# Full-height products in linear attention, later operands, and low parts of weights formed by accumulating transfers beside the key selection

## The chip, the cores and the metric

The kernel runs on one core of a Trainium2 chip. The metric is the device time of one execution in microseconds (us). In three runs the kernel before took 1966.81, 1968.53 and 1969.35 us; the median is 1968.53.

## The reference

Two transformer blocks are computed for 512 positions, in fp32. The change lies in the second block. Its input is normalized and multiplied by one wide weight matrix; the columns are q, k, v of sparse attention (qa, ka, va), the index queries and keys that select keys (qi, ki, wi), and q, k, v, the gates and the output gate of gated linear attention (qb, kb, vb, gdown, ogate).

```
score = einsum('bqhs,bqh->bqs', relu(q_idx . k_idx * c1), w_idx * c2)   # in blocks of 64 queries
_, sel = lax.top_k(score, 128)                                          # the key selection, 128 keys for each query
# gated linear attention, chunks of 64 positions, 4 heads, 64 key columns and 128 value columns each
q_in = q / 8 * exp(bcum);  k_in = k * exp(-bcum);  k_dec = k * exp(blast - bcum)
att  = tril(q_in . k_in) within a chunk
o    = att . v + q_in . state;   state = state * exp(blast) + k_dec^T . v
```

## The kernel before

**Products.** A weight product in fp32 is made of three (`mm3`): a tile of weights is split into a high part wh and a low part wl = raw - wh, and hi·hi (L160), hi·lo (L161) and lo·hi (L162) are accumulated in PSUM; the order of the operands on these lines makes L162 (L204 where tokens stand on the output's rows) the one that reads wl. `weights` (L167) loads a tile of 512 KB with an SP transfer into `raw`, ACT casts it to wh (L172), and a third engine subtracts (L173). raw, wh and wl have three buffers each, so a tile's buffers come back three tiles later. A tile feeds 24 products of 128 rows by 512 columns.

**The engine of the subtraction.** `low_engine["e"]` names it: VectorE (DVE), except from L1258 to L1267, during the key selection, where it is GpSimd (POOL).

**The key selection.** `topk_steps` makes index scores on TensorE (PE, L972, evacuated by ACT at L974 and weighted and added up by DVE at L977 and L979) and then runs rounds of max and match_replace on DVE (L989, L990) for three groups of 128 queries. Between its steps `bg.fill` takes steps of gemms out of a queue, in the order kb, vb, og, va, qk (`Feed`), so that PE has work while DVE selects. From the ninth step on, a generator, `gla_steps`, is advanced as well, one `next` for each step of the selection, as soon as the gemms that its last `yield` named are out of the queue.

**Linear attention.** Two heads share a tile: rows 0 to 63 belong to the one, rows 64 to 127 to the other. `gla_gates` makes the cumulated gates (L1072, L1074). `gla_operands(n)` makes q_in (in place, L1088), k_in and k_dec of pair n; `gla_turn(n)` transposes k_dec on PE (L1104) and copies it (L1106); `gla_inner(h)` makes the products inside chunks (L1135) and masks them; `gla_state` carries the states; `gla_out(h)` adds att·v (L1147, over 128 rows) and q_in·state (L1152, over the 64 rows of the head) in PSUM, in four blocks of one product of 128 columns and two of 64 (one in the first block).

**What sets the order.** The engines run their instructions in the order in which they are issued; the code is passed through a scheduler that orders each engine's instructions once, ahead of the run. A wait written after an instruction below holds everything behind it on that engine. Waits on DMASW are for transfers that POOL issues, those on DMAHW for transfers that SP issues.

Of the kernel before, what the change touches and what calls it, by code (L numbers as in the profile page):

```python
# [121 lines left out]
def build(tc, A, dump=None):  # L122
    nc = tc.nc
    with ExitStack() as es:
# [11 lines left out]
        def wtile(tag, shape, dt):  # L136
            return P.tile(shape, dt, tag=tag, name=tag, bufs=SLOTS[tag])
# [27 lines left out]
        low_engine = {"e": nc.vector}  # L165

        def weights(w, k0, kn, c0, ncol):  # L167
            raw = wtile("raw", [128, kn, ncol], F32)
            nc.sync.dma_start(raw, w[k0 * 128:(k0 + kn) * 128, c0:c0 + ncol].rearrange("(k p) n -> p k n", p=128))
            wh = wtile("wh", [128, kn, ncol], F32R)  # L170
            wl = wtile("wl", [128, kn, ncol], F32R)
            nc.scalar.copy(wh, raw)  # L172
            low_engine["e"].tensor_tensor(out=wl, in0=raw, in1=f(wh), op=ALU.subtract)  # L173
            return wh, wl
# [905 lines left out]
        def gla_operands(n, bc):  # L1080
            bl = small("bl", 8, bufs=2)
            nc.vector.tensor_copy(bl, bc[:, 63:T:64])
            eb = small("eb", 8, bufs=2)
            nc.scalar.activation(eb, bl, AF.Exp, scale=1.0 / 16)
            gl["eb", n] = eb
            e1 = new("t")
            nc.scalar.activation(e1, bc, AF.Exp, scale=1.0 / 16)
            nc.vector.scalar_tensor_tensor(out=qb[n], in0=qb[n], scalar=0.125, in1=e1, op0=ALU.mult, op1=ALU.mult)  # L1088
            e2 = new("t")
            nc.scalar.activation(e2, bc, AF.Exp, scale=-1.0 / 16)  # L1090
            kin = new("q")
            nc.vector.tensor_mul(kin, kb[n], e2)
            gl["k", n] = kin
            bc3 = bc.rearrange("p (c s) -> p c s", s=64)
            nc.vector.tensor_sub(bc3, bl[:, :, None].to_broadcast([128, 8, 64]), bc3)
            nc.scalar.activation(bc, bc, AF.Exp, scale=1.0 / 16)
            nc.vector.tensor_mul(kb[n], kb[n], bc)
# [30 lines left out]
                                                   in1=kv[rr, hh * 128:hh * 128 + 128], op0=ALU.mult, op1=ALU.add)  # L1128

        def gla_inner(h):  # L1130
            n, rr = h // 2, slice(64 * (h % 2), 64 * (h % 2) + 64)
            z = psum("r")
            for b in range(4):
                bs = slice(b * 128, b * 128 + 128)
                nc.tensor.matmul(z[:, bs], gl["k", n][rr, bs], qb[n][rr, bs], start=True, stop=True)  # L1135
            at = new("q")
            nc.gpsimd.memset(at, 0.0)
            nc.vector.copy_predicated(at, gl["mask"], z)
            gl["at", h] = at

        def gla_out(h):
            n, rr = h // 2, slice(64 * (h % 2), 64 * (h % 2) + 64)
            at = gl["at", h]
            o = psum("r")
            for b in range(4):
                bs = slice(b * 128, b * 128 + 128)
                nc.tensor.matmul(o[:, bs], vb[b][:, h * 128:h * 128 + 128], at[:, bs], start=True, stop=False)  # L1147
                for c in (2 * b, 2 * b + 1):
                    if c == 0:
                        continue  # L1150
                    s = gl["S", n][(c - 1) // 4][rr, ((c - 1) % 4) * 128:((c - 1) % 4) * 128 + 128]
                    nc.tensor.matmul(o[:, c * 64:c * 64 + 64], s, qb[n][rr, c * 64:c * 64 + 64], start=False,  # L1152
                                     stop=c == 2 * b + 1)
            oh = new("q")
            nc.scalar.copy(oh, o)
            gl["o", h] = oh
            sq = new("t")
            nc.scalar.activation(sq, o, AF.Square)
            st = psum("o")
            colsum(st, 0, [sq])  # L1160
            rc = small("rcg", 4, bufs=4)
            rsqrt_cols(rc, st[:, 0:4], 4, 1.0 / 128)
            gl["r", h] = rc
# [11 lines left out]
        def gla_steps():  # L1175
            bcs = []
            for _ in gla_gates(bcs):
                yield "start"
            glam = const(None, C_GLA, 512)
            gl["mask"] = small("glau", 512, U8)  # L1180
            nc.gpsimd.tensor_copy(out=gl["mask"], in_=glam)
            yield "kb"
            for n in range(2):
                gla_operands(n, bcs[n])
                yield "kb"
            for n in range(2):
                gla_turn(n)
                yield "kb"
            for h in range(4):
                gla_inner(h)  # L1190
                yield "vb"
            for c in range(7):
                for n in range(2):
                    gla_state(n, c)
                yield "vb"
            for h in range(4):
                gla_out(h)
                yield "og"
                if h > 0:
                    gla_norm(h - 1)  # L1200
            yield "og"
            gla_norm(3)
# [52 lines left out]
            for c in range(4):  # L1255
                yield from gemm(A["w_out_2"], 4, 256 * c, late, ev, n0=2 * c, k0w=4)
        bg.add("wo", residual())
        low_engine["e"] = nc.gpsimd  # L1258
        gla = gla_steps()
        wait = next(gla)  # L1260
        for i, us in enumerate(topk_steps()):
# [157 lines left out]
```

## Time and profile before

| what | value |
|---|---|
| median of three runs | 1968.53 us |
| the profiled execution | 1973.42 us |
| its span, from first to last instruction | 1971.7 us |
| mean granted TensorE clock | 0.978 of full speed |
| PE busy | 1893.1 us, 96% |
| DVE busy | 1071.8 us, 54% |
| ACT busy | 725.8 us, 37% |
| POOL busy | 315.9 us, 16% |

A busy PE is not PE at its best: its products take longer where the granted clock is lower, and a product that waits inside PE for the one before it counts as busy. The selection begins at about 1264 us, the first piece of `gla_out` runs at 1382 us, and the last head ends at about 1414 us.

### The profile page before, as it was taken

The page shows a single profiled execution, that of the slowest core. Times are in us where ns is not written, and L with a number is a line of the kernel's source. Part 1 is how long each engine was busy: PE and PEld are TensorE (multiplying, and loading weights), DVE is VectorE, ACT ScalarE, POOL GpSimd, SP SyncE. Part 2 cuts the span into 40 slices and gives each one's busy share as a digit, 9 for nine tenths or more (in the row PEclk, how much of TensorE's full clock was granted, in tenths as well). Part 3 has the DMA queues.
Part 4 walks back from the last instruction along what each step waited for, and adds up shares of the span by engine and source line. Part 5 has one row for each costly group of instructions (what it writes and reads, how often), then busy time and mean ns, then how long its engine had stood idle before and what let it go on. Part 6 is the DMA issues. An engine that isn't in the chain of part 4 may idle for free. (4 is left out here: it accounts for less than half of the span.)

```text
span 1971.7 us, 24556 instructions
## 1 busy us (share of the span) xinstructions
PE 1893.1 (96%) x9561; PEld 1572.9 (80%) x9561; DVE 1071.8 (54%) x1730; ACT 725.8 (37%) x1226; POOL 315.9 (16%) x357
## 2 busy tenths in 40 slices
PE   5889999999999999999999999979999899999998
PEld 4678887888889898888888888767878788888886
DVE  6788875645464554664443322587377653433222
ACT  3466654233323323343222223552256532322222
POOL 3232211112020302010000002332344200000000
PEclk8899999999999999999999999989899999999999
DMA  7612222443424243623323234232133123333222
GB/s 222 193 54 65 65 73 92 146 123 107 134 88 142 79 137 124 196 76 106 93 90 96 91 102 123 66 109 63 34 101 103 53 66 95 96 96 95 87 86 75
DMA packets 193520, 199.25 MB, mean 101 GB/s; under 512 B 9718, under 2 KB 178692, under 8 KB 193404
## 3 DMA queue, kind: packets, MB, share of 16 engines
q1 hardware_dynamic: 189920, 188.48, 31.2%
q0 software_dynamic: 3136, 9.08, 1.3%
q8 instruction: 75, 1.23, 0.3%
q14 instruction: 41, 0.34, 0.1%
q10 hardware_dynamic: 348, 0.13, 0.0%
HBM read 189.25 MB, written 9.99 MB: 101 GB/s over the span
## 5 line engine op out<-in xcount | busy, mean ns | idle before, releaser
L160 PE MATMUL ps_g<-p,wh 128*128 128x512 f32 (+1 forms) x1464 | 580.4, 399 | 9.5 <-ACT p L150 2.9
L161 PE MATMUL ps_g<-p,wh 128*128 128x512 f32 (+1 forms) x1464 | 577.3, 395 | 2.9 <-DVE p L405 2.9
L162 PE MATMUL ps_g<-p,wl 128*128 128x512 f32 (+1 forms) x1464 | 576.6, 394 | 0.0
L173 DVE TENSOR_TENSOR wl<-raw,wh 128x1024 fp32r<-128x1024 f32 (+1 forms) x262 | 325.7, 1243 | 448.3 <-ACT wh L172 447.1
L172 ACT CAST wh<-raw 128x1024 fp32r<-128x1024 f32 (+1 forms) x282 | 294.3, 1044 | 658.3 <-PE ps_g L161 373.2
L160 PEld LDWEIGHTS ps_g<-p,wh 128*128 128x128 f32 x1464 | 277.3, 190 | 74.6 <-issue 7.5
L161 PEld LDWEIGHTS ps_g<-p,wh 128*128 128x128 f32 x1464 | 278.1, 190 | 63.8 <-DVE p L405 3.6
L162 PEld LDWEIGHTS ps_g<-p,wl 128*128 128x128 f32 x1464 | 277.7, 190 | 63.2
L203 PE MATMUL ps_g<-wh,p 128*128 128x256 f32 x512 | 148.0, 289 | 1.6 <-ACT wh L172 1.5
L204 PE MATMUL ps_g<-wl,p 128*128 128x256 f32 x512 | 145.7, 285 | 1.2 <-DVE wl L173 1.2
L205 PE MATMUL ps_g<-wh,p 128*128 128x256 f32 x512 | 145.9, 285 | 0.0
L160 PE MATMUL ps_g<-q,wh 128*128 128x512 f32 (+1 forms) x368 | 141.7, 388 | 0.2 <-DVE p L1253 0.2
L162 PE MATMUL ps_g<-q,wl 128*128 128x512 f32 (+1 forms) x368 | 141.6, 385 | 0.0
L161 PE MATMUL ps_g<-q,wh 128*128 128x512 f32 (+1 forms) x368 | 141.5, 385 | 0.0
L203 PEld LDWEIGHTS ps_g<-wh,p 128*128 128x128 f32 x512 | 98.7, 193 | 3.0 <-ACT wh L172 1.9
L204 PEld LDWEIGHTS ps_g<-wl,p 128*128 128x128 f32 x512 | 98.8, 193 | 1.9 <-DVE wl L173 1.4
L205 PEld LDWEIGHTS ps_g<-wh,p 128*128 128x128 f32 x512 | 98.8, 193 | 0.1
L160 PEld LDWEIGHTS ps_g<-q,wh 128*128 128x128 f32 x368 | 69.1, 188 | 16.1 <-DVE p L1253 0.5
L162 PEld LDWEIGHTS ps_g<-q,wl 128*128 128x128 f32 x368 | 69.2, 188 | 15.0
L161 PEld LDWEIGHTS ps_g<-q,wh 128*128 128x128 f32 x368 | 69.2, 188 | 14.6
L150 ACT CAST q<-t 128x512 fp32r<-128x512 f32 (+1 forms) x68 | 39.2, 582 | 87.3 <-DVE t L880 48.8
L319 DVE SCALAR_TENSOR_TENSOR adaacc<-raw,cact,adaacc 128x256 f32<-128x256 f32 x112 | 53.8, 481 | 24.9 <-DMA raw<-in_w_ada 23.1
(373 smaller groups left out, 2601.0 us busy)
## 6 DMA issues: line engine op xcount, KB each, us to landing
raw<-in_w_in SPq DMA_DIRECT2D x108, 512.0 KB, 3.6
raw<-in_w_ffn_in SPq DMA_DIRECT2D x44, 512.0 KB, 3.5
raw<-in_w_ada SPq DMA_DIRECT2D x32, 512.0 KB, 3.4
raw<-in_w_ffn_gate SPq DMA_DIRECT2D x22, 512.0 KB, 3.7
raw<-in_w_ffn_up SPq DMA_DIRECT2D x22, 512.0 KB
raw<-in_w_ffn_down SPq DMA_DIRECT2D x22, 512.0 KB, 3.7
raw<-in_w_ffn_out SPq DMA_DIRECT2D x19, 512.0 KB, 3.4
raw<-in_w_proj_ret SPq DMA_DIRECT2D x16, 512.0 KB, 3.3
```

The lines of the kernel that those rows point to most:

```text
L150: nc.scalar.copy(hi, src)
L160: nc.tensor.matmul(ps, lh, rh, start=start, stop=False)
L161: nc.tensor.matmul(ps, lh, rl, start=False, stop=False)
L162: nc.tensor.matmul(ps, ll, rh, start=False, stop=stop)
L172: nc.scalar.copy(wh, raw)
L173: low_engine["e"].tensor_tensor(out=wl, in0=raw, in1=f(wh), op=ALU.subtract)
L203: nc.tensor.matmul(o, xh[:, ts], wh[:, i], start=k == 0 and t % 2 == 0, stop=False)
L204: nc.tensor.matmul(o, xh[:, ts], wl[:, i], start=False, stop=False)
L205: nc.tensor.matmul(o, xl[:, ts], wh[:, i], start=False, stop=k == KD - 1 and t % 2 == 1)
L319: nc.vector.scalar_tensor_tensor(out=acc, in0=w, scalar=c, in1=acc, op0=ALU.mult, op1=ALU.add)
```

## The change

Three things are changed. In the part of the program in which POOL subtracted, a low part is now formed so: ACT writes wh, ACT writes -wh into the buffer of wl, and a transfer issued by POOL adds raw to it. q_in of a pair is no longer one tile in place but two tiles of 128 rows, one for each head, in which the 64 rows of the other head are set to zero by POOL; `gla_inner` and `gla_out` then contract over all 128 rows. And `gla_steps` yields once more ahead of each `gla_operands`, so that operands, transposes and all that follows come one step of the selection later for the first pair and two for the second.

```diff
--- before.py
+++ after.py
@@ -165,6 +165,16 @@
         low_engine = {"e": nc.vector}
 
         def weights(w, k0, kn, c0, ncol):
+            if low_engine["e"] is None:
+
+                raw = wtile("raw", [128, kn, ncol], F32)
+                nc.sync.dma_start(raw, w[k0 * 128:(k0 + kn) * 128, c0:c0 + ncol].rearrange("(k p) n -> p k n", p=128))
+                wh = wtile("wh", [128, kn, ncol], F32R)
+                wl = wtile("wl", [128, kn, ncol], F32R)
+                nc.scalar.copy(wh, raw)
+                nc.scalar.activation(wl, f(wh), AF.Copy, scale=-1.0)
+                nc.gpsimd.dma_start(wl, raw, accum_op=ALU.add)
+                return wh, wl
             raw = wtile("raw", [128, kn, ncol], F32)
             nc.sync.dma_start(raw, w[k0 * 128:(k0 + kn) * 128, c0:c0 + ncol].rearrange("(k p) n -> p k n", p=128))
             wh = wtile("wh", [128, kn, ncol], F32R)
@@ -1085,7 +1095,12 @@
             gl["eb", n] = eb
             e1 = new("t")
             nc.scalar.activation(e1, bc, AF.Exp, scale=1.0 / 16)
-            nc.vector.scalar_tensor_tensor(out=qb[n], in0=qb[n], scalar=0.125, in1=e1, op0=ALU.mult, op1=ALU.mult)
+            for hh in range(2):
+
+                r, o = slice(64 * hh, 64 * hh + 64), slice(64 - 64 * hh, 128 - 64 * hh)
+                qz = gl["q", 2 * n + hh] = new("q")
+                nc.gpsimd.memset(qz[o], 0.0)
+                nc.vector.scalar_tensor_tensor(out=qz[r], in0=qb[n][r], scalar=0.125, in1=e1[r], op0=ALU.mult, op1=ALU.mult)
             e2 = new("t")
             nc.scalar.activation(e2, bc, AF.Exp, scale=-1.0 / 16)
             kin = new("q")
@@ -1128,18 +1143,18 @@
                                                    in1=kv[rr, hh * 128:hh * 128 + 128], op0=ALU.mult, op1=ALU.add)
 
         def gla_inner(h):
-            n, rr = h // 2, slice(64 * (h % 2), 64 * (h % 2) + 64)
+            n, qz = h // 2, gl["q", h]
             z = psum("r")
             for b in range(4):
                 bs = slice(b * 128, b * 128 + 128)
-                nc.tensor.matmul(z[:, bs], gl["k", n][rr, bs], qb[n][rr, bs], start=True, stop=True)
+                nc.tensor.matmul(z[:, bs], gl["k", n][:, bs], qz[:, bs], start=True, stop=True)
             at = new("q")
             nc.gpsimd.memset(at, 0.0)
             nc.vector.copy_predicated(at, gl["mask"], z)
             gl["at", h] = at
 
         def gla_out(h):
-            n, rr = h // 2, slice(64 * (h % 2), 64 * (h % 2) + 64)
+            n, qz = h // 2, gl["q", h]
             at = gl["at", h]
             o = psum("r")
             for b in range(4):
@@ -1148,8 +1163,8 @@
                 for c in (2 * b, 2 * b + 1):
                     if c == 0:
                         continue
-                    s = gl["S", n][(c - 1) // 4][rr, ((c - 1) % 4) * 128:((c - 1) % 4) * 128 + 128]
-                    nc.tensor.matmul(o[:, c * 64:c * 64 + 64], s, qb[n][rr, c * 64:c * 64 + 64], start=False,
+                    s = gl["S", n][(c - 1) // 4][:, ((c - 1) % 4) * 128:((c - 1) % 4) * 128 + 128]
+                    nc.tensor.matmul(o[:, c * 64:c * 64 + 64], s, qz[:, c * 64:c * 64 + 64], start=False,
                                      stop=c == 2 * b + 1)
             oh = new("q")
             nc.scalar.copy(oh, o)
@@ -1181,6 +1196,7 @@
             nc.gpsimd.tensor_copy(out=gl["mask"], in_=glam)
             yield "kb"
             for n in range(2):
+                yield "kb"
                 gla_operands(n, bcs[n])
                 yield "kb"
             for n in range(2):
@@ -1255,7 +1271,7 @@
             for c in range(4):
                 yield from gemm(A["w_out_2"], 4, 256 * c, late, ev, n0=2 * c, k0w=4)
         bg.add("wo", residual())
-        low_engine["e"] = nc.gpsimd
+        low_engine["e"] = None
         gla = gla_steps()
         wait = next(gla)
         for i, us in enumerate(topk_steps()):
```

Line numbers behind `weights` grow by 10, behind `gla_operands` by 15: L972 becomes L982, L1104 becomes L1119, L1135 becomes L1150, L1147 and L1152 become L1162 and L1167. The negation is L175, the accumulating transfer L176.

What the change does to the order of instructions is seen at three places. The first is PE at the beginning of the selection, with the first tile of the kb gemm (p are its activations). Before:

```order
L160 MATMUL ps_g<-p,wh 128x512 [waits DVE_49]
L161 MATMUL ps_g<-p,wh 128x512
L162 MATMUL ps_g<-p,wl 128x512 [waits Pool_49]
...
L161 MATMUL ps_g<-p,wh 128x512
L162 MATMUL ps_g<-p,wl 128x512
L160 MATMUL ps_g<-p,wh 128x512 [waits DVE_49,PE_49]
L972 MATMUL ps_z<-q 128x512 [waits DVE_49]
L972 MATMUL ps_r<-q 128x512 x2
L161 MATMUL ps_g<-p,wh 128x512
L960 MATMUL ps_o<-eye,q 128x8 [waits DVE_49]
L960 MATMUL ps_o<-eye,q 128x8 x2
L162 MATMUL ps_g<-p,wl 128x512
```

and now:

```order
L160 MATMUL ps_g<-p,wh 128x512 [waits DVE_49]
L161 MATMUL ps_g<-p,wh 128x512
L160 MATMUL ps_g<-p,wh 128x512 [waits DVE_49,PE_49]
L161 MATMUL ps_g<-p,wh 128x512
L982 MATMUL ps_z<-q 128x512 [waits DVE_49]
L982 MATMUL ps_r<-q 128x512 x2
...
L1225 MATMUL ps_o<-k,rel 8x384 [waits DMASW5_49,DMASW1_49,DVE_49]
L982 MATMUL ps_z<-q 128x512 [waits DVE_49]
L1069 MATMUL ps_o<-q,k 128x512 [waits DMASW6_49,DVE_49]
L160 MATMUL ps_g<-p,wh 128x512 [waits Activation_49]
L161 MATMUL ps_g<-p,wh 128x512
L162 MATMUL ps_g<-p,wl 128x512 [waits DMASW0_49]
```

Before, L162 stood third and waited for POOL's subtraction; now four products that do not read wl come first, then the index products and the two small products of L1225 and L1069, and the first L162 behind them waits for the transfer (DMASW0).

The second place is POOL in the same part (gd, far and gt are tables of the position bias). Before:

```order
L1215 DMA far<-gd 128x8x1 [waits DMASW2_49,DMASW0_49]
L1217 DMA gt<-gd 1032x1x384 [waits DMASW3_49]
L173 TENSOR_TENSOR wl<-raw,wh 128x1024 [waits DMAHW2_49,PE_49,Activation_49]
L236 DMA k<-in_consts 128x512 [waits DMASW6_49,DMASW4_49,PE_49]
L173 TENSOR_TENSOR wl<-raw,wh 128x1024 [waits DMAHW3_49,PE_49,Activation_49]
L173 TENSOR_TENSOR wl<-raw,wh 128x1024 [waits DMAHW4_49,PE_49,Activation_49]
L1277 DMA k<-gt 128x2x256 [waits DMASW3_49,DMASW1_49,DVE_49]
L1181 CAST glau<-k 128x512 [waits DMASW4_49]
L1277 DMA k<-gt 128x2x256 [waits Pool_49]
L173 TENSOR_TENSOR wl<-raw,wh 128x1024 [waits DMAHW5_49,PE_49,Activation_49]
L1137 MEMSET q 128x512 x4
L173 TENSOR_TENSOR wl<-raw,wh 128x1024 [waits DMAHW6_49,Activation_49]
```

and now:

```order
L176 DMA wl<-raw 128x1024 [waits DMASW3_49,DMAHW0_49,Activation_49,Pool_49]
L1231 DMA far<-gd 128x8x1 [waits DMASW4_49,DMASW2_49]
L1233 DMA gt<-gd 1032x1x384
L176 DMA wl<-raw 128x1024 [waits DMAHW1_49,DMASW6_49,Activation_49]
L176 DMA wl<-raw 128x1024 [waits DMASW7_49,DMASW0_49,DMAHW2_49,PE_49,Activation_49]
...
L176 DMA wl<-raw 128x1024 [waits DMASW3_49,DMASW1_49,DMAHW3_49,PE_49,Activation_49]
L1293 DMA k<-gt 128x2x256 [waits DMASW5_49,DVE_49]
...
L176 DMA wl<-raw 128x1024 [waits DMASW6_49,DMAHW4_49,DMASW4_49,Activation_49]
L1102 MEMSET q 64x512 x2
L176 DMA wl<-raw 128x1024 [waits DMASW7_49,DMAHW5_49,PE_49,Activation_49]
L1102 MEMSET q 64x512 x2
```

Subtractions are now issues of transfers; those of the first tiles stand among the transfers of gd, far and gt on the same queue, the third one behind gt, and the zeros of q_in (L1102) stand between later ones.

The third place is PE around the first transposes of linear attention, in the gemm of vb. Before:

```order
L203 MATMUL ps_g<-wh,p 128x256
L204 MATMUL ps_g<-wl,p 128x256 [waits Pool_49]
L205 MATMUL ps_g<-wh,p 128x256
L203 MATMUL ps_g<-wh,p 128x256
L204 MATMUL ps_g<-wl,p 128x256
L205 MATMUL ps_g<-wh,p 128x256
L1104 MATMUL ps_o<-eye,q 128x128 [waits DVE_49]
L1104 MATMUL ps_o<-eye,q 128x128 x3
```

and now, the first three rows at the place where the transposes stood and the others where they stand:

```order
L213 MATMUL ps_g<-wh,p 128x256
L214 MATMUL ps_g<-wl,p 128x256 [waits DMASW4_49]
L215 MATMUL ps_g<-wh,p 128x256
...
L213 MATMUL ps_g<-wh,p 128x256 [waits Activation_49]
L214 MATMUL ps_g<-wl,p 128x256 [waits DMASW5_49]
L215 MATMUL ps_g<-wh,p 128x256
L1119 MATMUL ps_o<-eye,q 128x128 [waits DVE_49]
L1119 MATMUL ps_o<-eye,q 128x128 x3
```

The transposes stand 46 rows later in PE's order (row 6275 in place of 6229; those of the second pair 6298 in place of 6252), behind the first product that waits for one tile more.

## Rows read from the trace of the kernel before

**Rows 1.** The page: busy us, share of the span and instructions of each engine.

```profile
PE 1893.1 (96%) x9561; PEld 1572.9 (80%) x9561; DVE 1071.8 (54%) x1730; ACT 725.8 (37%) x1226; POOL 315.9 (16%) x357
```

**Rows 2.** Waits of PE, 1255 to 1470 us: us in total, times, longest.

```profile
PE ps_z L972 <- ACT t L974: 8.1, 1, 8.1
PE ps_o L1104 <- DVE p L1106: 3.3, 1, 3.3
```

**Rows 3.** Stretches: length, busy us (instructions) of the engines, clock, DMA share, GB/s.

```profile
1275.00:1289.00 14.00, 14.00 (x32) 7.70 (x31) 5.10 (x9) 6.67 (x11) 7.83 (x6) 0.51 0.48 130
1300.00:1320.00 20.00, 11.86 (x49) 9.44 (x48) 20.00 (x33) 8.80 (x19) 9.97 (x7) 0.74 0.42 119
...
1392.00:1408.00 16.00, 16.00 (x84) 14.70 (x83) 2.63 (x6) 2.79 (x5) 2.87 (x3) 0.69 0.11 33
```

**Rows 4.** Timeline of PE: start us, us, engine line operation out<-in.

```profile
1382.34 0.38 PE L1147 MATMUL ps_r<-q,p 128*128 128x128 f32 x2
...
1386.02 0.50 PE L160 MATMUL ps_g<-p,wh 128*128 128x512 f32 x1
...
1387.51 0.95 PE L268 MATMUL ps_o<-ones,t 128*128 128x1 f32 x8
1388.32 0.48 PE L160 MATMUL ps_g<-p,wh 128*128 128x512 f32 x1
...
1336.96 1.16 PE L1135 MATMUL ps_r<-q 64*128 64x128 f32 x8
```

**Rows 5.** Groups of POOL, whole span: count, then busy us, mean ns, idle before.

```profile
L173 POOL TENSOR_TENSOR wl<-raw,wh 128x1024 fp32r<-128x1024 f32 x20 | 48.6, 2432 | 85.7 <-ACT wh L172 77.3 <-DVE q L956 8.3
```

**Rows 6.** Timeline of POOL, 1262 to 1335 us.

```profile
1299.43 2.40 POOL L173 TENSOR_TENSOR wl<-raw,wh 128x1024 fp32r<-128x1024 f32 x1 [13.80 <-ACT wh L172]
1301.79 0.58 POOL L236 DMA_DIRECT2D k<-in_consts  x1
1302.39 5.29 POOL L173 TENSOR_TENSOR wl<-raw,wh 128x1024 fp32r<-128x1024 f32 x2
```

**Rows 7.** Timeline of DVE, 1298 to 1330 us.

```profile
1297.54 0.69 DVE L1072 TENSOR_TENSOR t<-t 128x512 f32<-128x512 f32 x1 [2.09 <-ACT t L1069]
...
1299.93 2.99 DVE L1074 TENSOR_TENSOR_SCAN q<-k,t 128x512 f32<-128x512 f32 x1
...
1303.43 2.06 DVE L979 SCALAR_TENSOR_TENSOR q<-t,wi,q 128x384 f32<-128x384 f32 x1
...
1306.07 2.16 DVE L1072 TENSOR_TENSOR t<-t 128x512 f32<-128x512 f32 x1
...
1308.76 1.20 DVE L1074 TENSOR_TENSOR_SCAN q<-k,t 128x512 f32<-128x512 f32 x1
...
1311.90 0.59 DVE L979 SCALAR_TENSOR_TENSOR q<-t,wi,q 128x384 f32<-128x384 f32 x1
...
1322.48 2.51 DVE L1092 TENSOR_TENSOR q<-q,t 128x512 f32<-128x512 f32 x1 [0.74 <-ACT q L1040]
```

**Rows 8.** Timeline of ACT, 1262 to 1278 us.

```profile
1263.63 1.05 ACT L172 CAST wh<-raw 128x1024 fp32r<-128x1024 f32 x1
...
1274.30 1.05 ACT L172 CAST wh<-raw 128x1024 fp32r<-128x1024 f32 x1
```

**Rows 9.** DMA issues: count, KB each, median us from issue to landing.

```profile
yspill<-p POOLq DMA_DIRECT2D x8, 256.0 KB, 3.3
...
gt<-gd POOLq DMA_DIRECT2D x1, 1548.0 KB, 10.8
```

**Rows 10.** Timeline of PE, 1266 to 1283 us.

```profile
1268.23 0.40 PE L160 MATMUL ps_g<-p,wh 128*128 128x512 f32 x1
...
1270.80 0.40 PE L162 MATMUL ps_g<-p,wl 128*128 128x512 f32 x1
1272.55 0.47 PE L160 MATMUL ps_g<-p,wh 128*128 128x512 f32 x1 [1.35 <-DVE q L933]
...
1280.04 0.63 PE L160 MATMUL ps_g<-p,wh 128*128 128x512 f32 x1
```

## The prediction

> **What bounds the kernel now.** Read the page's share of busy time first [rows 1]: TensorE (PE) works 96% of the span, so time is won only where PE stands still, runs at its lower clock level, or spends longer on its products than it need. The change touches only the second block from the start of the key selection (about 1264 us) to the end of gated linear attention (about 1414 us); the rest of the program keeps its instructions. So the second view is the list of PE's waits in that stretch [rows 2]. Two of them stand where the change works. PE waits 8.1 us once in front of L972, the index products, for ACT's L974, which evacuates scores that VectorE (DVE) has not yet consumed; and 3.3 us once at L1104, the transposes of linear attention's k, for DVE's copies at L1106. The third view is a table of stretches [rows 3]. In 1275 to 1289 PE has work the whole time but a granted clock of 0.51, its lower level (1.2 of 2.4 GHz), after gaps at the start of the selection such as the one of 1.35 us before 1272.55 [rows 10]. In 1300 to 1320 DVE is busy 20.00 of 20.00 us: there the selection rounds set the pace and PE waits for them. In 1392 to 1408 PE is busy throughout, waits for nobody, and is granted 0.69. That stretch follows the first two heads of `gla_out`; what PE did before the clock fell was mostly full products with these short 64-row ones between them. The fourth view, the timelines, gives durations.
>
> **Products over all rows.** The pieces of `gla_out` for one head run from 1382.34 to 1386.02, where the next gemm product starts: 3.68 us [rows 4], for four products of 128 columns at L1147 and seven chunks of state products at L1152. L1152 contracts over 64 partitions and L1147 over 128, and they alternate. A run of fp32 products that do not alternate is L268: eight from 1387.51 to the next product at 1388.32, 0.10 us each, though with one column [rows 4]. An fp32 product counts twice in the trace: 8 for L1147 and 14 for L1152, 22 in a head. At 0.10 these take 2.2 us, so a head could lose 1.45 us and four heads 5.8. `gla_inner` (L1135, eight of 64 rows, 1.16 us before PE goes on at its pace) against L268 (0.95 for eight) adds 0.2 to 0.3 a head, some 1.1 in all. The spacing is worth 6.9 us, bounds 6.9 and 0, since no row shows the 128-row form of these very products, and L268's narrowness may flatter it. I take the upper end, because the products that follow one another without a change of rows are the nearest row. The clock of 1392 to 1408 has lost 16 x 0.31 = 5.0 us; if products that use half of the rows are what let it fall, full rows give most of it back. I take 4, bounds 0 and 5.0. Together 10.9.
>
> The trace shows a head's 3.68 us and not why it is long. The Trainium skill ("TensorE: Matmul & The Clock Gate", section "Why this matters for your kernels") says that one product with a small contraction takes as long as a full one, and that only several tiles running side by side gain; by that the spacing term would be 0. Its page "TensorEngine Tiling (Array Packing)", section "Key Properties", says that a change of tiling mode drains the engine; by that the alternation is the cost and the 6.9 stands. The alternating 22 at 0.17 us against 0.10 for L268 agree with the second, so I follow it and keep the first as a rival.
>
> **GpSimd's subtractions go.** Twenty at 2.43 us leave POOL [rows 5]. POOL is not on the path; DVE, which they slow, is. While POOL subtracts at 1299.43 and 1302.39 (two, 5.29 us) [rows 6], DVE's L1074 takes 2.99 us where its twin takes 1.20, L979 2.06 against 0.59, L1072 2.16 against 0.69 [rows 7]: 1.8 + 1.5 + 1.5 = 4.7 us before the 8.1 us wait ends. L1092 at 1322.48 is a `tensor_tensor` of the shape of L1072 and takes 2.51 against 0.69, which is 1.8 before the 3.3 us wait.
>
> **The longer way of a low part.** Cast, negation and an accumulating transfer replace cast and subtraction. The negation has the shape of the cast: 1.05 us [rows 8], 20 of them 21 us on ACT, which in 1300 to 1320 works 8.80 of 20 us [rows 3], so it is hidden there. POOL's issue costs 0.58 us (L236) [rows 6] in place of 2.43. No row shows an accumulation between two SBUF tiles. Bounds for its landing: 3.3 us for 256 KB and 10.8 us for 1548 KB, both on POOL's queue [rows 9]. Between them on a line, 512 KB give 4.8 us, and 7.8 if reading source and destination counts as 1024 KB; I take 6. Per tile that is 1.05 + 1.05 + 0.6 + 6 = 8.7 us from raw data to low part. A tile feeds 24 products at 0.233 us ((1270.80 - 1268.23) / 11) [rows 10], 5.6 us, and with three buffers of each kind two tiles, 11.2 us, cover it. So in the steady part it costs nothing; where cover lacks is the start and, perhaps, the third tile, whose transfer the order puts behind the 1548 KB of `gt` in POOL's queue: 0 if the queue overlaps them, up to about 6 if not; I take 2.
>
> At the start there is no cover. ACT is full of evacuations: the second cast comes 10.7 us after the first [rows 8], and in the new order the negation of tile one stands about there. Its transfer can leave at 1276 and lands at 1282. PE before has run 19 products of the first tile by 1280.04 (the twelfth at 1270.80) [rows 10]; in the new order it runs only four that need no low part, then waits at L162. Fifteen products are late: 15 x 0.233 = 3.5 us, or 7.0 at the lower level. The clock there is 0.51 [rows 3], so I take 6. What absorbs it: PE comes 6 us later to the 8.1 us wait, DVE 4.7 us earlier, together over 8.1, so the wait ends (-8.1) and the start's delay is paid (+6). If DVE's relief failed, the wait would only shrink by the 6 us and both would cancel. After this wait the next late thing is DVE itself, whose rounds are still 20 of 20 there.
>
> **Operands later and in halves.** Two more `scalar_tensor_tensor` of 64 rows: 2 x 0.68 = 1.4 us more on DVE (L1088's shape, as L1072's 0.69 [rows 7]; a half-height instruction is assumed to cost the same). Against the relief of 1.8 that leaves 0.4; but the two additional steps put each L1104 some 46 rows later in PE's order, more cover than the 3.3 us wait. New waits in front of `gla_inner` for POOL's zeros (four half tiles) have a POOL that has lost 48.6 us of work as cover. I count -1.8 of the 3.3, bounds -3.3 and +1.4.
>
> **Sum.** -6.9 - 4 + 6 - 8.1 - 1.8 + 2 = -12.8 us on the profiled execution (1973.4 us, span 1971.7): 1960.6. That execution lies 4.9 us above the median of the runs, 1968.5; with the same distance the median becomes 1955.7, forecast 1956.
>
> **Rivals.** (1) *The transfers are late for every tile, slower.* PE would meet its first low-part product before the landing. Three buffers turn over in three tiles, 16.8 us; a turn needs 5.6 (products) + 2.9 (cast, negation with its issue) + landing, so it decides from a landing of 8.3 us. At 10.8 a turn loses 2.5 us, 20 tiles lose 17, and each wait brings some of the lower clock, as after the gaps before 1275 (0.51): with 6 us for that +23, 1956 + 23 = 1979. For it: the accumulation moves twice the bytes, and `gt` shares the queue. Against: 3.3 us for a spill on that queue. POOL issued L236 at 1301.79 in 0.58 us, while DVE was fully busy [rows 3, 6]. The skill's page "SBUF — State Buffer", section "Who interferes with whom", says that a DMA issued by GpSimd can be starved by DVE's use of their shared port; that would bring this rival about in just the 20 us where DVE never rests, and the 0.58 us is against it. Chance 0.15.
> (2) *The wider products gain nothing.* Each takes what a 64-row product takes and the clock falls as before: 1956 + 10.9 = 1967. For it: L1152 and L1147 alternate columns and accumulation too, not rows alone. Chance 0.13.
> (3) *The start is paid and the waits stay.* The rounds on DVE go no faster, or other work waits for them: -10.9 + 6 = -4.9, 1964. For it: DVE is at 20.00 of 20.00 and gets two more instructions. Chance 0.13.
> (4) *Everything goes*: -6.9 - 5.0 - 8.1 - 3.3 = -23.3, with the start's late products filling other gaps: 1945. Chance 0.10.
> The forecast keeps 0.49, with a range of its own of 1951 to 1961.
>
> A measurement tells 0.2% (3.9 us) from no change: under 1964.6 is faster, over 1972.5 slower. Faster: the forecast 0.49, (4) 0.10, about 0.09 of (3), 0.03 of (2) = 0.71. Slower: nearly all of (1) = 0.15. Same: 0.14. The range 1947 to 1974 leaves out most of (1) and half of (4).
>
> **What would show it.** In the new profile a head of `gla_out` takes about 2.3 us instead of 3.68, and the clock between its heads stays near 1; if it takes 3.6, the product step is wrong. L1074 at 1.2 us throughout shows DVE's relief. The wait before L982 for ACT is gone or below 2 us, and one of some 3 to 7 us appears at the first L162, for the transfer. The accumulation lands in 4 to 8 us; above 8.3 us PE waits at L162 and L214 again and again, and the forecast is wrong. ACT's own queue must not become what L162 waits for beyond the first tile.

## The result, and the profile after

Four runs of the changed kernel took 1955.99 to 1957.54 us, median 1956.9; four of the kernel before, 1966.81 to 1969.35, median 1968.44. The ratio is 0.9938 (95% interval 0.9926 to 0.9950): faster by 11.5 us, where 12.5 were forecast (1956 us, range 1947 to 1974). A second measurement, told below, gave 0.9923 (0.9902 to 0.9943).

The profiled executions lie further apart: 1973.42 before and 1956.69 after, 16.7 us. That of before is 5.0 us above its median, that of after 0.2 below. Both traces are compared below, so what they show adds up to 16.7 and not to 11.5. All of it lies in the part that was changed: from the first product of the kb gemm to the first score product (L493, L503 now) of the attention that follows linear attention, PE takes 189.4 us before and 172.0 after, 17.4 less, while 0.2 us are lost ahead of this stretch and 0.6 behind it.

```profile
1457.65 0.34 PE L493 MATMUL ps_z<-q 128*128 128x128 f32 x2
```

```profile
1268.43 0.40 PE L160 MATMUL ps_g<-p,wh 128*128 128x512 f32 x1
...
1440.40 0.34 PE L503 MATMUL ps_z<-q 128*128 128x128 f32 x2
```

The first row is that of before, whose stretch begins at 1268.23 [rows 10]. In which stage the other executions of the kernel before were shorter than the profiled one is not recorded.

The page of the changed kernel, with busy time, share and instructions of each engine, against [rows 1]:

```profile
span 1955.0 us, 24601 instructions
...
PE 1879.9 (96%) x9561; PEld 1563.7 (80%) x9561; DVE 1062.4 (54%) x1732; ACT 748.5 (38%) x1248; POOL 287.9 (15%) x361
```

PE's share is unchanged; it lost 13 us of busy time with the same number of instructions. ACT has gained 23 us and 22 instructions: the 20 negations, and two more loads of its function tables (`ACT_TABLE_LOAD`, 1.28 us each; 9 in the trace instead of 7).

The waits of PE, 1255 to 1470 us, against [rows 2] (us in total, times, longest):

```profile
PE ps_z L982 <- ACT t L984: 6.6, 3, 3.1
PE ps_g L160 <- DVE q L943: 3.7, 1, 3.7
...
PE ps_r L982 <- ACT t L984: 1.2, 1, 1.2
PE ps_z L982 <- DVE q L964: 0.5, 1, 0.5
```

The wait for ACT's L984 (L974 before) is not gone: with 6.6 + 1.2 = 7.8 us it is nearly what it was, 8.1. The wait at the transposes of linear attention is gone, and so is one of before at L160, behind linear attention, that the rows ahead of the prediction do not have:

```profile
PE ps_g L160 <- DVE q L475: 2.6, 1, 2.6
```

No wait for a transfer appears.

Four stretches, against [rows 3] (length, busy us of PE, PEld, DVE, ACT, POOL, then clock, DMA share and GB/s):

```profile
1300.00:1320.00 20.00, 14.30 (x42) 10.60 (x43) 16.83 (x34) 13.47 (x27) 3.54 (x5) 0.66 0.59 155
1320.00:1340.00 20.00, 20.00 (x162) 19.47 (x161) 14.14 (x30) 8.48 (x12) 7.03 (x12) 1.00 0.73 151
...
1392.00:1408.00 16.00, 16.00 (x140) 15.79 (x139) 7.03 (x16) 6.47 (x11) 6.67 (x6) 1.00 0.26 62
1408.00:1438.00 30.00, 30.00 (x163) 25.64 (x162) 22.94 (x58) 16.19 (x22) 7.09 (x8) 1.00 0.74 168
```

DVE has 3.2 us free in 1300 to 1320. From 1320 to 1438 PE works without a gap and the clock is 1.00, its upper level, in every stretch read. The work that stood in 1392 to 1408 before, at a clock of 0.69, stands 6 to 12 us earlier now, and earlier, too, stands the work that follows the wait of 2.6 us, at 1423 in place of 1439. There the clock was 0.66 before:

```profile
1438.00:1443.00 5.00, 3.60 (x10) 2.93 (x11) 3.62 (x9) 2.75 (x4) 2.37 (x1) 0.66 0.00 0
```

The timeline of PE, against [rows 4]:

```profile
1378.71 0.38 PE L1162 MATMUL ps_r<-q,p 128*128 128x128 f32 x2
1378.93 0.33 PE L1167 MATMUL ps_r<-q 128*128 128x64 f32 x2
1379.10 0.44 PE L1162 MATMUL ps_r<-q,p 128*128 128x128 f32 x2
1379.38 0.56 PE L1167 MATMUL ps_r<-q 128*128 128x64 f32 x4
1379.77 0.44 PE L1162 MATMUL ps_r<-q,p 128*128 128x128 f32 x2
...
1381.09 0.48 PE L160 MATMUL ps_g<-p,wh 128*128 128x512 f32 x1
...
1339.81 1.05 PE L1150 MATMUL ps_r<-q 128*128 128x128 f32 x8
1340.62 0.37 PE L213 MATMUL ps_g<-wh,p 128*128 128x256 f32 x1
```

A head of `gla_out` takes 2.38 us instead of 3.68, and `gla_inner`'s eight products 0.81 us where the next product followed after 1.08. The DVE timeline, against [rows 7], and the landing of the new transfers, against [rows 9]:

```profile
1302.21 1.21 DVE L1084 TENSOR_TENSOR_SCAN q<-k,t 128x512 f32<-128x512 f32 x1
...
1305.11 0.68 DVE L1082 TENSOR_TENSOR t<-t 128x512 f32<-128x512 f32 x1
...
1306.36 1.22 DVE L1084 TENSOR_TENSOR_SCAN q<-k,t 128x512 f32<-128x512 f32 x1
```

```profile
wl<-raw POOLq DMA_DIRECT2D x20, 512.0 KB, 5.6
```

L1084 no longer takes 2.99 us, nor L1082 2.16. A low part lands 5.6 us after its issue, the median of the 20 (6 was taken).

### The profile page after: what moved, and what is told of

Read it like the earlier page. It is cut to its first block, busy times and chain, and to the rows that moved or that the text cites. A ratio compares the mean times of both kernels' runs of the same rounds, so it can differ in the third digit from the quotient of the medians.

```text
span 1955.0 us, 24601 instructions
## 1 busy us (share of the span) xinstructions
PE 1879.9 (96%) x9561; PEld 1563.7 (80%) x9561; DVE 1062.4 (54%) x1732; ACT 748.5 (38%) x1248; POOL 287.9 (15%) x361
## 5 line engine op out<-in xcount | busy, mean ns | idle before, releaser
L160 PE MATMUL ps_g<-p,wh 128*128 128x512 f32 (+1 forms) x1464 | 579.4, 399 | 9.3 <-DVE q L943 3.7
L162 PE MATMUL ps_g<-p,wl 128*128 128x512 f32 (+1 forms) x1464 | 575.5, 394 | 0.0
L182 ACT CAST wh<-raw 128x1024 fp32r<-128x1024 f32 (+1 forms) x262 | 273.2, 1043 | 630.5 <-PE ps_g L161 358.3
L160 PEld LDWEIGHTS ps_g<-p,wh 128*128 128x128 f32 x1464 | 276.4, 190 | 75.1 <-issue 8.3
L162 PEld LDWEIGHTS ps_g<-p,wl 128*128 128x128 f32 x1464 | 277.2, 189 | 63.4
L160 PE MATMUL ps_g<-q,wh 128*128 128x512 f32 (+1 forms) x368 | 141.7, 388 | 0.2 <-DVE p L1269 0.2
L162 PE MATMUL ps_g<-q,wl 128*128 128x512 f32 (+1 forms) x368 | 141.5, 385 | 0.0
L160 PEld LDWEIGHTS ps_g<-q,wh 128*128 128x128 f32 x368 | 69.1, 188 | 16.1 <-DVE p L1269 0.6
L162 PEld LDWEIGHTS ps_g<-q,wl 128*128 128x128 f32 x368 | 69.2, 188 | 15.0
```

What stands on the lines that cost most here:

```text
L160: nc.tensor.matmul(ps, lh, rh, start=start, stop=False)
L162: nc.tensor.matmul(ps, ll, rh, start=False, stop=stop)
```

## The experiments

All were timed in five rounds beside the kernel before; chips differ, so ratios are compared. A loss or gain in us behind a ratio is worked out from it.

Executions also differ ahead of the change: the first product of the kb gemm starts between 1264.9 and 1269.9 us in the thirteen traces, though no edit lies ahead of it. So the table has the stretch of each trace as well, from that product to the first score product, as above. It is one execution of each kernel; the two of the change agree within 0.1 us.

| kernel | ratio | stretch, us |
|---|---|---|
| before | 1 | 189.4 |
| the change, twice | 0.9938, 0.9923 | 172.0, 172.1 |
| the products alone | 0.9935 | 177.3 |
| the low parts alone | 0.9961 | 185.3 |
| the change with products of 64 rows | 0.9965 | 184.4 |
| the change, operands at their old step | 0.9906 | 171.4 |
| the change, subtraction on POOL | 0.9954 | 178.3 |
| the change, transfer twice | 1.0018 | 191.1 |
| the change, first tile on POOL | 0.9882 | 167.0 |
| the change, first three tiles on POOL | 0.9904 | 167.5 |
| the change, first tile on POOL, operands at their old step | 0.9897 | 167.2 |
| the change without negation | 0.9938 | 169.7 |

**The products alone.** Edits to the changed kernel:

```diff
             for n in range(2):
-                yield "kb"
                 gla_operands(n, bcs[n])
...
-        low_engine["e"] = None
+        low_engine["e"] = nc.gpsimd
```

> Only the full-height products (two tiles of q_in with zeros, products over 128 rows); low parts are subtracted by POOL as before, operands at their old step. The prediction's theory: -6.9 us of spacing and -4 of clock in the heads of gla_out, +1.4 for two more DVE instructions in front of the 3.3 us wait at L1104, so 1958 to 1960 us. Rival, the wider products gain nothing and the change won by the low parts: 1968 to 1970. Between them, the spacing is won and the clock is not: about 1963, with a head at 2.4 us and a stretch of some 16 us at a granted clock near 0.7 still there.

Measured: 0.9935 (0.9919 to 0.9950), -12.8 us; the stretch gives -12.1. Each head takes 2.37 or 2.38 us, and the clock of 1392 to 1408 is 1.00. Spacing and clock come together; the rival falls. Its waits are nearly those of before: 8.1 at L982, and 4.4 at L1119 where it was 3.3.

**The low parts alone.** The reverse: products over 64 rows, q_in in place, no additional yield.

> Only the low parts by negation and accumulating transfer; products over 64 rows, operands at their old step. The prediction's theory: +6 at the start, +2 for the third tile, -8.1 for the wait at the index products, up to -1.8 at L1119: -2, so about 1966.5 us, and heads of gla_out still 3.7 us. Rival, the change won by relieving DVE of POOL: about 1957 to 1959. Second rival, negations on a full ACT replace what DVE gives back: 1968 or above, with waits for ACT's L984 in sum as long as the 8.1 us before.

Measured: 0.9961 (0.9947 to 0.9975), -7.7 us, where -2 was expected: more than the theory gave, less than the first rival; the stretch gives -4.1. Heads take 3.7 us again, one 6.48 at the lower clock. No wait at the transposes is left, and none at L160 for L485 (2.6 us at 1439 before). The second rival's waits are there, 7.3 + 1.2 = 8.5 us for ACT's L984, but not its time.

**The height of the products alone.** The changed kernel, with both products over the head's 64 rows (`rr`, a slice of rows that the edit brings back):

```diff
...
-                nc.tensor.matmul(z[:, bs], gl["k", n][:, bs], qz[:, bs], start=True, stop=True)
+                nc.tensor.matmul(z[:, bs], gl["k", n][rr, bs], qz[rr, bs], start=True, stop=True)
...
-                    s = gl["S", n][(c - 1) // 4][:, ((c - 1) % 4) * 128:((c - 1) % 4) * 128 + 128]
-                    nc.tensor.matmul(o[:, c * 64:c * 64 + 64], s, qz[:, c * 64:c * 64 + 64], start=False,
+                    s = gl["S", n][(c - 1) // 4][rr, ((c - 1) % 4) * 128:((c - 1) % 4) * 128 + 128]
+                    nc.tensor.matmul(o[:, c * 64:c * 64 + 64], s, qz[rr, c * 64:c * 64 + 64], start=False,
```

> The whole change, zeros and halves of q_in too, but gla_inner and gla_out contract over the 64 rows of the head again: only the height of the products differs from the changed kernel (1956.9 us). The prediction's theory: 10.9 us are lost, about 1968. Only the spacing counts and the clock does not: about 1963. Rival, the height of a product costs nothing: 1957.

Measured: 0.9965 (0.9953 to 0.9977) of the kernel before, 1965.82 us; the change itself was measured at 1956.9 and, on another chip, 1957.56. By ratios and medians the height is worth 5 to 9 us, by the stretch 12.4 (184.4 against 172.0), where 10.9 were expected. The stretches and the first head show both halves of it:

```profile
1380.00:1392.00 12.00, 12.00 (x66) 10.11 (x65) 3.36 (x9) 3.57 (x5) 1.93 (x2) 0.86 0.26 63
1392.00:1408.00 16.00, 16.00 (x87) 14.96 (x86) 3.35 (x10) 2.79 (x5) 2.81 (x3) 0.68 0.26 61
```

```profile
1379.31 0.38 PE L1162 MATMUL ps_r<-q,p 128*128 128x128 f32 x2
1379.62 0.43 PE L1167 MATMUL ps_r<-q 64*128 64x64 f32 x2
1379.98 0.49 PE L1162 MATMUL ps_r<-q,p 128*128 128x128 f32 x2
1380.40 0.66 PE L1167 MATMUL ps_r<-q 64*128 64x64 f32 x4
1380.99 0.49 PE L1162 MATMUL ps_r<-q,p 128*128 128x128 f32 x2
...
1383.16 0.79 PE L160 MATMUL ps_g<-p,wh 128*128 128x512 f32 x1
```

With 64 rows the head takes 3.85 us and the clock falls, to 0.68 here; with 128 rows, in the same order of instructions, 2.38 and 1.00. In the three traces with 64-row products the clock in this stretch is 0.69 (before), 0.54 (low parts alone) and 0.68, in the ten with 128 rows 1.00.

The rows also show where the spacing is lost: at the changes of height, not at each 64-row product. From the start of one L1167 (x2, as an fp32 product counts twice) to the next L1162 it is 0.36 us, from that of two (x4) 0.59, so one more costs 0.23; with 128 rows it is 0.17 and 0.39, and one more costs 0.22. The head has eight changes of height, which add 0.09 to 0.22 us each in the kernel before, 1.30 in all.

**The change once more.**

> The changed kernel once more, beside the three below on one chip, since its parts alone came to -12.8 and -7.7 us of the kernel before and add up to -20.5, while the whole was measured at -11.5. If the parts add, the ratio is about 0.990; if they overlap, 0.994 again.

Measured: 0.9923 (0.9902 to 0.9943), 1957.56 us. The interval leaves 0.990 out by little and holds 0.994; by the ratios, whether the parts add is not settled. In the stretches they nearly do: -12.1 and -4.1 make -16.2, the whole has -17.4 and -17.3.

**Operands at their old step.** The changed kernel without the additional yield.

> The changed kernel without the additional yields: operands at their old step. Theory: the yields are worth at most 1.8 us, since DVE is relieved already and no wait at L1119 is seen either way: as the change within 2 us. Rival: the operands' DVE work again stands in front of the transposes, and a wait of 3 to 4 us comes back at L1119: +3 us against the change.

Measured: 0.9906 (0.9886 to 0.9927), 1953.53 us, the change 1957.56 beside it: no loss, and the rival's wait does not come back, its list has no L1119. The yields win nothing.

**The subtraction back on POOL.** `low_engine["e"] = nc.gpsimd` in the changed kernel, with the yields.

> The changed kernel with POOL's subtraction instead of negation and transfer: full-height products and later operands alone. Theory (relief of DVE and start nearly cancel, -2 for the low parts): about 2 us above the change. Rival, taken from the two runs of single parts: the transfers are worth 7 us, so 7 above the change, with the 8.1 us wait at the index products back. Third: the later operands cost nothing and take away the 4.4 us wait at L1119 seen with the products alone, so it equals the change.

Measured: 0.9954 (0.9936 to 0.9973), 1961.83 us, 4 us above the change by the medians, 6 by the ratios and by the stretch: nearer to the rival's 7 than to the theory's 2. The waits:

```profile
PE ps_z L982 <- ACT t L984: 7.7, 2, 5.3
PE ps_o L1119 <- DVE p L1121: 5.3, 1, 5.3
PE ps_g L160 <- DVE q L485: 2.6, 1, 2.6
```

The third theory falls: the later step does not take the wait at L1119 away. What removes it is that POOL no longer subtracts: DVE's L1112, which stands ahead of these copies, takes 2.79 us here and 0.68 in the change. That PE only comes later in the change is not the reason. With the first tile alone on POOL (below) it reaches the second pair's transposes 63.5 us after the first kb product and does not wait; here it gets there at 64.1 and waits 5.3.

**The transfer twice.**

```diff
                 nc.gpsimd.dma_start(wl, raw, accum_op=ALU.add)
+                nc.gpsimd.dma_start(wl, raw, accum_op=ALU.add)
```

> The changed kernel with each accumulating transfer done twice in a row, the second after the first has landed, so that a low part comes 5 to 6 us later (the values added twice are wrong). The prediction's cover argument: a turn of three tiles is 16.8 us and needs 5.6 + 2.9 + landing; at 11 to 12 us of landing it loses 2.7 to 3.7 a turn, 18 to 25 us for 20 tiles, and PE waits at L162 and L214 for the transfer. Rival, there is more cover than the three buffers suggest (the products of other tiles and of linear attention stand between): under 8 us, most of it at the start.

Measured: 1.0018 (1.0006 to 1.0030), 1974.41 us, 16.9 above the change, just below the 18 to 25; the stretch gives 19. PE now waits for transfers:

```profile
PE ps_g L215 <- DMA wl<-raw: 8.8, 6, 2.7
PE ps_g L162 <- DMA wl<-raw: 6.0, 5, 2.0
PE ps_g L160 <- DVE q L944: 3.7, 1, 3.7
```

Eleven waits, 14.8 us: the cover is about what three buffers give, and one landing of 5.6 us fits in it.

**The first tile on POOL.** The first tile after the switch is subtracted by POOL, all others go by the transfer:

```diff
-        low_engine = {"e": nc.vector}
+        low_engine = {"e": nc.vector, "n": 1}
...
-            if low_engine["e"] is None:
+            if low_engine["e"] is None and low_engine["n"] > 0:
+                low_engine["n"] -= 1
+                low = nc.gpsimd
+            else:
+                low = low_engine["e"]
+            if low is None:
...
-            low_engine["e"].tensor_tensor(out=wl, in0=raw, in1=f(wh), op=ALU.subtract)
+            low.tensor_tensor(out=wl, in0=raw, in1=f(wh), op=ALU.subtract)
```

> The changed kernel, but the first tile of weights after the switch has its low part subtracted by POOL as before; all others go by the transfer. The prediction's theory: the start's +6 us come back, because the first fifteen products run where they ran before: about 1951 us. Rival: PE then only comes earlier to the waits for ACT's L984 in 1296 to 1310, which grow by as much, and nothing is won: 1956 to 1958.

Measured: 0.9882 (0.9863 to 0.9900), 1950.19 us, faster than both kernels. The waits for ACT, and that of the start:

```profile
PE ps_z L987 <- ACT t L989: 4.4, 3, 3.1
...
PE ps_g L160 <- DVE q L948: 1.4, 1, 1.4
...
PE ps_r L987 <- ACT t L989: 0.9, 1, 0.9
```

The rival falls: the start's wait goes from 3.7 back to 1.4 us, and those behind it shrink from 7.8 to 5.3 instead of growing.

**The first three tiles on POOL, and the first one with operands at their old step.** The same edit with `"n"` at 3, and with 1 and without the additional yield.

> The changed kernel with the first three tiles subtracted by POOL. Against the first one only (1950): theory A takes two more negations from ACT in front of the waits for L984, 1947 to 1949. Theory B: DVE's instructions are stretched beside POOL's subtractions again, 1.5 us each, while nothing is given back: 1951 to 1953.

> The first tile on POOL and the operands at their old step, without the additional yields. The run without the yields was as fast as the change or faster by up to 3 us; so 1947 to 1950 here, and the fastest of all that were tried. Rival: with the start's products back, PE comes earlier to L1119 and meets DVE's copies: a wait of 2 to 4 us there, 1952 to 1954.

Measured: 0.9904 (0.9890 to 0.9917) and 0.9897 (0.9883 to 0.9910), medians 1949.75 and 1948.11 us. Neither can be told from the first tile alone; one tile is enough.

**No negation.** wl is filled by a plain transfer of raw, ACT writes only wh.

> The changed kernel with the low part replaced by a plain transfer of the raw tile, without the negation and without adding (wl holds raw, so values are wrong): 20 x 1.05 us leave ACT, the transfer stays. Its start is ordered as in the kernel with the first tile on POOL (1950), so the two differ by 19 negations on ACT. Theory A, the waits for ACT's L984 that are left are ACT's own, since it was busy 10.90 of 11 us in 1289 to 1300: they shrink and 3 to 5 us are won, 1945 to 1947. Theory B, these waits are DVE's rounds seen through ACT (DVE frees the tiles that L984 writes): nothing is won, 1950.

Measured: 0.9938 (0.9924 to 0.9951), 1956.37 us: slower than with the first tile on POOL, which neither theory gave. The order moved with it: waits for L983 (L984 in the change) fall to 1.7 us, as theory A has it, but two others of 3.8 and 3.9 us appear, for ACT's L1049, which stands behind an ACT instruction that itself waits 1.69 us for DVE, and for DVE's L1106. DVE is busy 19.20 of 20 us in 1300 to 1320. So without the negations ACT no longer ends these waits, and DVE takes its place; what the negations alone cost the change is left open.

## Why the prediction was right, and where it was not

**The products (-10.9), right in both halves.** Heads went from 15.0 us together to 9.5, -5.5 where -5.8 was forecast; `gla_inner` 4 x 0.27 = -1.1 as forecast; the clock of 1392 to 1408 gave back all 5.0, where 4 was taken. The height alone was changed in one experiment and brought both back. Rival (2) is out. What is shown is that products over half the rows, in runs that alternate with full ones, cost here, and that the spacing is lost at the changes of height. This is the place that the Trainium skill's page "TensorEngine Tiling (Array Packing)", section "Key Properties", gives: changing the tiling mode drains the engine. The trace agrees with the place (1.30 us for eight changes) and does not show the draining itself. What it is about the height that lets the clock fall, the rows in use or the pauses at the changes, was not measured apart.

**GpSimd's relief of DVE, right in mechanism, in another place.** DVE's stretched instructions are back to 1.21 and 0.68 us. But it was to end the 8.1 us wait, and did not: the waits for L984 are 7.8 us, in four pieces (8.2 with a short one for wh between). The relief paid off later: the 3.3 + 0.6 us at L1104 went (-1.8 was counted), and so did 2.6 us at 1439 for DVE's L475, with the lower clock behind it, which the prediction had not seen. Both stay in the runs with POOL's subtraction and are gone in the one with the low parts alone.

**The start (+6) and the wait (-8.1): the step that failed.** It is the prediction's "PE comes 6 us later to the 8.1 us wait, DVE 4.7 us earlier, together over 8.1, so the wait ends", and with it the sentence that the negations are hidden on ACT because it works 8.80 of 20 us in 1300 to 1320. Three things went another way.

First, the wait of before was not for scores that DVE had yet to consume. ACT's L974 stood in ACT's order behind an exponential of the cumulated gates (L1087), and ACT stood idle there for DVE's second L1074 (the rows are those of before):

```profile
1310.06 0.63 ACT L1087 ACTIVATE t<-q 128x512 f32<-128x512 f32 x1 [4.27 <-DVE q L1074]
...
1311.11 0.36 ACT L974 ACTIVATE t<-ps_z 128x256 f32<-128x256 f32 x1
```

```profile
1311.53 1.13 PE L972 MATMUL ps_z<-q 96*128 96x256 f32 x2 [8.14 <-ACT t L974]
```

Second, the relief ended ACT's waiting, but ACT's own work took its place. The second L1084 ends at 1307.6 us where L1074 ended at 1310.0, 2.4 us earlier and not 4.7. The list of waits has none of ACT's there any more, and it works nearly throughout (12.29 of 12.40 us):

```profile
1297.00:1309.40 12.40, 4.24 (x11) 2.33 (x10) 9.90 (x19) 12.29 (x23) 2.43 (x4) 0.69 0.91 214
```

```profile
1295.93 1.28 ACT L1077 ACT_TABLE_LOAD   x1
...
1298.25 1.28 ACT L1079 ACT_TABLE_LOAD   x1
```

```profile
1298.28 0.44 PE L982 MATMUL ps_r<-q 96*128 96x384 f32 x1 [1.19 <-ACT t L984]
1301.09 0.44 PE L982 MATMUL ps_z<-q 96*128 96x384 f32 x1 [2.37 <-ACT t L984]
...
1309.36 0.58 PE L982 MATMUL ps_z<-q 96*128 96x256 f32 x1 [1.16 <-ACT t L984]
```

The two table loads that are new stand directly ahead of the first two waits: the scheduler now orders the gates' L1077 and L1079 in turn, where before both L1067 came ahead of both L1069. With the first tile on POOL there are 7 loads again, and these two waits are 0.33 and 0.94 us.

Third, the scheduler has moved PE's work too: the last of the index products there is PE's 6392nd product in the trace where it was the 6415th, so some 23 gemm products that ran ahead of them now come behind. PE's first wait for L984 begins at 1297.1 us instead of 1303.4, and the last ends at 1309.4 instead of 1311.5. PE thus arrives at the waits earlier, with less done, and not later. The start itself shows in the timeline of PE, against [rows 10]:

```profile
1268.66 0.40 PE L161 MATMUL ps_g<-p,wh 128*128 128x512 f32 x1
1272.76 0.77 PE L160 MATMUL ps_g<-p,wh 128*128 128x512 f32 x1 [3.70 <-DVE q L943]
1273.32 0.63 PE L161 MATMUL ps_g<-p,wh 128*128 128x512 f32 x1
...
1280.93 0.80 PE L160 MATMUL ps_g<-p,wh 128*128 128x512 f32 x1
...
1281.95 0.63 PE L162 MATMUL ps_g<-p,wl 128*128 128x512 f32 x1
```

Four products, then the next at 1280.93, as forecast; but L162 does not wait for the transfer. PE waits 3.7 us for DVE's L943, which frees a PSUM buffer, and 0.5 for L964, in place of 1.35 and 1.26 us. The cost of this start is what the first tile on POOL saves: 4.5 to 5.4 us between the profiled executions (1952.22 against 1956.69 and 1957.63), 5.0 in the stretch, about 7 between medians. So the +6 was near in size and wrong in place: 1.6 us of it are waits at the start, 2.5 are the waits for L984, which go from 5.3 to 7.8. Rival (3), the start paid and the waits staying, is what happened here; it was priced at 1964 us, and savings that the prediction had not counted made up for it.

**The cover of three buffers, right.** No wait for a transfer in the change (+2 for the third tile was not needed, although `gt` lands in 13.5 us), and eleven of them when the landing was doubled. Rival (1) was a real danger, at a doubled landing. Its 2.9 us for cast, negation and issue are 2.7 by the rows it names; with the 0.87 us that an issue of L176 took they are 3.0, so its limit of 8.3 us for the landing hardly moves (8.2).

**The yields**: the prediction counted their 46 rows as cover against the 3.3 us wait. They were not needed: without them that wait does not come back, and the stretch is 171.4 us against 172.0.

**The sum.** In the traces: products -6.6, clock of 1392 to 1408 -5.0, start +1.6 of waiting (4.2 against 2.6 us), L1104 -3.9, 1439 -2.6 and -1.7 of clock, 1320 to 1340 -1.8 of clock, 1300 to 1320 +1.6: -18.4, with the wait's -0.3 -18.7, against 17.4 in the stretch and 16.7 between the two executions; a wait in a stretch of lower clock is counted in both. The prediction's -12.8 was 3.9 too small for these two executions. Its other assumption, that the changed kernel's profiled execution also lies 4.9 us above its median, was wrong by nearly as much the other way (it lies 0.2 below). So the forecast is closer to the result than its working deserves: its hitting 1956 within 1 us is luck, its products are not.

## What to carry to other kernels

Where short products over half the rows alternate with full ones, zeros in the other rows can be worth more than they cost: look at the time lost at each change of height and at the clock behind the stretch. When a step gets a longer chain, look at its first instance apart: steady cover hid it everywhere but there in this kernel, and leaving that one instance on the old way brought another 5 us in the stretch, on top of 17.4. And a wait is not ended by shortening what it waits for if the engine between is filled up, or if the scheduler moves work from before the wait to behind it: follow the releasing engine's own queue in the stretch where the wait lies (its mean busy time over 20 us hid this one), and count the rows ahead of the wait in the new order before subtracting.

## What was not expected of the hardware

The lower clock in the middle of a stretch in which PE was busy 16.00 of 16.00 us: 0.69 before, 0.68 with half-height products in the changed kernel, 0.54 with the low parts alone, 1.00 with full height. The cost of 64-row products stands at the change of height, 0.09 to 0.22 us each, and not at the products. And an accumulating transfer of 512 KB between SBUF tiles lands in 4.7 to 5.6 us (the medians of these runs), against 3.2 for a plain one of the same size on the same queue in the run without negation.
